# The full-width products of a transformer layer: 544 rows as 272 + 272 columns in place of 256 + 288

## The chip, the cores and the metric

The kernel runs on one core of a Trainium2 chip. The metric is the device time of one execution in microseconds (us); the time before is the median of three runs. Engines: TensorE (PE; its weight loads are shown apart as PEld), VectorE (DVE), ScalarE (ACT), GpSimd (POOL) and SyncE (SP), which issues most transfers.

## The reference

One layer of a model is computed for two inputs: a prompt of 512 rows and a sample of 8 sequences with 4 new rows each, 544 rows of 1024 features in all. Cut to what matters:

```python
def layer_forward(h, lp, conv_buf, ssm_h0, attn_fn, mem_k, mem_v):
    u = rmsnorm(h, lp['ffn1_pre_g'])
    h = h + 0.5 * rmsnorm(swiglu(u, lp['ffn1_wg'], lp['ffn1_wu'], lp['ffn1_wd']), lp['ffn1_post_g'])
    u = rmsnorm(h, lp['mix_pre_g'])
    z, xbc, dt_raw, q, k, v, qi, ki, wi, g_ssd, g_att = jnp.split(u @ lp['w_in'], IN_OFFSETS, axis=-1)
    y_ssd, new_conv, new_ssm = ssd_branch(z, xbc, dt_raw, ...)     # state-space branch
    y_att = attn_fn(q, k, v, qi, ki, wi)                           # sparse attention
    merged = (jax.nn.sigmoid(g_ssd) * (y_ssd @ lp['w_br_ssd'])
              + jax.nn.sigmoid(g_att) * (y_att @ lp['w_br_att']))
    h = h + rmsnorm(merged @ lp['w_out'], lp['mix_post_g'])
    u = rmsnorm(h, lp['mem_pre_g'])
    h = h + rmsnorm(mem_attend(u, lp['w_mq'], mem_k, mem_v) @ lp['w_mo'], lp['mem_post_g'])
    u = rmsnorm(h, lp['ffn2_pre_g'])
    h = h + 0.5 * rmsnorm(swiglu(u, lp['ffn2_wg'], lp['ffn2_wu'], lp['ffn2_wd']), lp['ffn2_post_g'])
    return h, (k, v, ki, new_ssm, new_conv)
```

All values are 32-bit floats. Nearly all arithmetic is in the products of `u` (or of the hidden layer, or of a branch) with a weight matrix.

## The kernel before

Activations lie feature-major: 128 features on the partitions, the T = 544 rows along the free axis (columns 0 to 511 the prompt, 512 to 543 the sample). A product with a weight matrix is made of tiles of 128 output features. For precision each operand is kept as two parts, high (`uh`, `wh`) and low (`ul`, `wl`), and a product is the sum of three: high by high, low by high, high by low.

`weights` (line 243) loads a part of a weight matrix through SyncE's queue into one of three raw buffers `wr`, ScalarE makes the high part `wh` (line 262) and VectorE or GpSimd the low part `wl` (line 263); there are two buffers of each. `mm` (line 275) makes one tile of a product: for each of its KT blocks of 128 input features, for each of the three pairs of parts, it issues one matmul per entry of `outs` (line 294). With `half=None` that is all 544 rows in two matmuls that go to a PSUM tile named `pg`; with `half` 0 or 1 it is rows 0 to 255 or 256 to 543 (`HALF`, line 21) in one matmul, into a tile named `pgh`. Every matmul has its own weight load in the instruction stream. `mm` is a generator: it yields an estimate of TensorE's time, 0.68 us per two blocks and entry of `outs`, by which `weave` (line 97) chooses whose instructions are emitted next; the emitted order is each engine's order.

Products by halves are used where a norm or a residual bounds two stages, so that one half can go on while the other is finished: the first six tiles of each feed-forward's up part, the last part of its down product, the first columns of `w_in`, and `w_out`, `w_mq`, `w_mo`. Full-width products are all the rest: most of the feed-forwards (lines 584, 585, 593), and of `w_in` (lines 727, 742, 993, 1115, 1140), `w_br_att` (line 1600) and `w_br_ssd` (line 1625). What reads a full-width result takes it whole: VectorE (`g`, lines 553 and 556; `y`, line 1601; `gt`, line 1626; `zt`, line 1118) or ScalarE (`y`, line 594; `th`, line 995; `CB`, line 1143 and others). The operands of full-width products are written in whole rows, or, at the head of a feed-forward and of the mixing stage, in the two halves of `HALF`, the second half by a generator that ends before the full-width products begin.

Of the kernel before, what the change touches and what calls it, by code (L numbers as in the profile page):

```python
# [14 lines left out]
PSUM = bass.MemoryType.PSUM  # L15
DRAM = bass.MemoryType.DRAM
P = 128
T = 544          # 512 prompt rows, then 32 of the sample
TP = 512
HA = 256         # the two halves of the rows: 0..255 and 256..543  # L20
HALF = ((0, 256), (256, 288))
D = 1024
# [7 lines left out]
def consts():  # L30
    """constants that depend on shapes alone"""
    a = np.arange
# [16 lines left out]
    # sample indexer; partitions (b, seg, t) with seg = pgh * 2 + c2  # L49
# [7 lines left out]
    # rows (c2, pgh, t, h); cols (pgh', c2', t')  # L57
# [3 lines left out]
    # rows (b4, t, h); cols (half, b', t')  # L61
# [35 lines left out]
def weave(*gens, extra=()):  # L97
    """emit streams side by side, the first the most urgent; each yields the tensor engine's time for what it has
    emitted, with the time until its next step can run where that is later, or WAIT for a flag; extra: streams
    that go on elsewhere when the others have ended"""  # L100
    now, idle = 0.0, 0
    live = [[g, 0.0] for g in (*gens, *extra)]
    while any(x[0] in gens for x in live):
        s = next((x for x in live if x[1] <= now), None)
        if s is None:
            s = min(live, key=lambda x: x[1])
            now = s[1]
        try:
            v = next(s[0])
        except StopIteration:  # L110
            live.remove(s)
            idle = 0
            continue
        if v is WAIT:
            idle += 1
            assert idle < 10000, "a wait that nothing ends"
            s[1] = now + 0.3
            continue
        idle = 0
        c, d = v if isinstance(v, tuple) else (v or 0.0, 0.0)  # L120
        now += c
        s[1] = now + d
# [38 lines left out]
class Net:  # L161
# [42 lines left out]
    def params(self):  # L204
        """gains and convolution parameters, feature on partitions"""
# [35 lines left out]
    WB = 2  # L241

    def weights(self, key, parts, KT, lo_eng=None):
        """parts: DRAM views [K, c]; -> hi, lo [P, KT, W] with hi + lo the weights"""
        nc, wp = self.nc, self.wp
        if key in self.wcache and self.wcount - self.wcache[key][0] < self.WB:
            return self.wcache[key][1]
        W = sum(p.shape[1] for p in parts)
        n = KT * W
        assert n <= 2048  # L250
        hi = wp.tile([P, 2048], F32R, tag="wh", name="wh", bufs=self.WB)
        lo = wp.tile([P, 2048], F32R, tag="wl", name="wl", bufs=self.WB)
        for k0, k1 in ((0, (KT + 1) // 2), ((KT + 1) // 2, KT)):
            raw = wp.tile([P, 1024], F32, tag="wr", name="wr", bufs=3)
            rv = raw[:, :(k1 - k0) * W].rearrange("p (k c) -> p k c", c=W)
            c = 0
            for p in parts:
                w = p.shape[1]
                nc.sync.dma_start(rv[:, :, c:c + w], p[k0 * P:k1 * P].rearrange("(k q) c -> q k c", q=P))
                c += w  # L260
            s, r = slice(k0 * W, k1 * W), raw[:, :(k1 - k0) * W]
            nc.scalar.copy(hi[:, s], r)  # L262
            (lo_eng or nc.vector).tensor_tensor(lo[:, s], r, hi[:, s].bitcast(F32), op=ALU.subtract)  # L263
        v = lambda t: t[:, :n].rearrange("p (k c) -> p k c", k=KT)
        self.wcache[key] = (self.wcount, (v(hi), v(lo)))
        self.wcount += 1
        return self.wcache[key][1]
# [7 lines left out]
    def mm(self, w, xs, c0, m=P, half=None):  # L275
        """one m-tile of weights.T @ x; half None: [m, T], else [m, rows of the half]"""
# [3 lines left out]
        if half is None:  # L280
            ps = self.pg.tile([P, 1024], F32, tag="pg", name="pg")
            outs = [(ps[:m, 256:512], 0, 256), (ps[:m, 512:800], 256, 288)]
            res = ps[:m, 256:800]
# [22 lines left out]
    def rsqrt(self, y, x, xh, t):  # L306
        """y = x ** -0.5 by Newton steps from a guess by the exponent"""
# [9 lines left out]
    def rms(self, sqs, inv_n, pool):  # L317
        """sqs: tiles [P, T] whose sum over tiles and partitions is the sum of squares
        -> rsqrt(mean + eps) on every partition, [P, rows of the prompt] and [P, rows of the sample] in PSUM"""
# [33 lines left out]
    def bound(self, half, sq, post_g, pre_g, rt=None):  # L353
        """hT += rms(y) * post_g, then u = rms(hT) * pre_g in two parts, on one half; sq: sum of squares of y;
        with rt, u goes without the rows' factor, which is left there for what is made of u"""
# [32 lines left out]
    def rms_h(self, acc, half):  # L388
        """as rms, for squares [P, rows of the half]"""
# [17 lines left out]
    def spread(self, y, half):  # L407
        """a factor by row, [P, blocks], on every partition, [P, rows of the half]"""
# [12 lines left out]
    def load_x(self, xp):  # L421
        """the rows, with the gains and the first weights of the feed-forward between the halves"""
# [16 lines left out]
    def load_T(self, half):  # L439
        """one half of x, feature-major; u without the rows' factor, and that"""  # L440
# [42 lines left out]
    def row_norm(self, x, scratch, pool):  # L483
        """rows of x [P, 2, D] over their root mean square"""
# [10 lines left out]
    def turn_rows(self, x, hi, lo, g):  # L495
        """[P, 2, D] times g, feature-major in two parts"""
# [10 lines left out]
    def memory_kv(self, mp):  # L507
        """-> the normed memory, then a piece for each of the weights' parts"""
# [28 lines left out]
    def ffn(self, nm, tail, lead, side=None, pieces=(), rt=None):  # L537
        """u -> y with hT += ... by tail(half, sq); lead: generator that completes u on half 1; side: a stream beside,
        pieces: streams that use the weights' buffers; rt: the factor of u's rows, if it is not in u"""
# [77 lines left out]
    def key_T(self):  # L617
# [4 lines left out]
        # pages of (b, pg16) in two halves  # L622
# [28 lines left out]
    def mix(self, lead):  # L651
# [28 lines left out]
        def outs(c):  # L680
            """weights and, per m-tile, (column, size, target)"""
# [88 lines left out]
    def out_rows(self, xT, n, out_p, out_s, pool, tag="orow"):  # L770
        """[n, T] feature-major -> rows of the outputs"""
# [14 lines left out]
    def dt_part(self, dw, ap):  # L786
        """step sizes, decays and their sums"""
# [28 lines left out]
        # softplus(x) = max(x, 0) + 2 atanh(e / (2 + e)), e = exp(-|x|)  # L816
# [16 lines left out]
        # prompt: sums within a chunk, [t, (c, h)]  # L833
# [21 lines left out]
        # sample; its rows three times over  # L855
# [32 lines left out]
        # d_skip by (h2, p)  # L888
# [14 lines left out]
    def sample_scores(self, qiT, kiT, dw):  # L903
# [8 lines left out]
        # indexer queries, block-diagonal over the two halves  # L912
# [9 lines left out]
        # head weights  # L922
# [15 lines left out]
        # new keys  # L938
# [87 lines left out]
    def prompt_att(self, kT, kx, V, qT, bias, g2, ready, wp):  # L1026
        """key groups 2 gp + g2"""
# [81 lines left out]
    def ssd_z(self, g):  # L1109
        """2 silu(z)"""  # L1110
# [11 lines left out]
    def ssd_x(self, g):  # L1122
        """x, B and C after the convolution"""
# [41 lines left out]
    def ssd_y(self, g, z):  # L1165
# [3 lines left out]
        # prompt  # L1169
# [37 lines left out]
        # sample; three copies of the rows for the products of the parts  # L1207
# [24 lines left out]
        # states of the prompt  # L1232
# [12 lines left out]
        # sample: states, feature-major, and their part of y; new states  # L1245
# [44 lines left out]
        # y  # L1290
# [41 lines left out]
    def conv_rows(self):  # L1332
        """last rows of the convolution's input"""
# [16 lines left out]
    def sample_select(self):  # L1350
# [17 lines left out]
        # threshold: the largest value that at least 256 of a query's candidates reach, two bits at a time in the  # L1368
        # floats' order; with the sign known a step turns the same bits of the float itself
# [32 lines left out]
        # rows in the pools  # L1402
# [16 lines left out]
        # new keys: row 65536 + j  # L1419
# [12 lines left out]
        # a query's list: its four lists end to end, each a run that starts so that its first entry falls in place  # L1432
# [29 lines left out]
    def sample_att(self):  # L1462
# [15 lines left out]
        def rows(st, v, q8):  # L1478
            """the keys or values of a query; the gathers run ahead"""
# [10 lines left out]
        for st in range(4):  # L1490
            # queries: [(g2, d), gp, (b, t), 2 x 16 heads], zero but for the heads of g;
            # tile kq holds heads 2 kq, 2 kq + 1 in its two halves; they read group kq // 2
# [79 lines left out]
    def att_in(self):  # L1572
        """y of the attention into the operands' place"""
# [15 lines left out]
    def att_out(self):  # L1589
        """B and its gate"""  # L1590
# [13 lines left out]
    def merge(self, h_d, rest):  # L1604
        """A with its gate and B, as the operands of w_out"""
# [27 lines left out]
    def project(self, name, post_g, pre_g, side=None, extra=()):  # L1633
        """u @ w, then its norm, residual and the next norm; half 1 of that is returned as a generator"""
# [18 lines left out]
    def mem(self):  # L1653
# [15 lines left out]
        def turn(out, mk):  # L1669
            """[256 m in 2 tiles, 1024] -> [P, 8, 256 m]"""  # L1670
# [8 lines left out]
        def soft(ps):  # L1679
            """softmax of ps / 16 over the free axis"""  # L1680
# [70 lines left out]
        def sample():  # L1751
            # rows (b, h, t)
            psS = self.pg.tile([P, 1024], F32, tag="pg", name="psS")[:, :256]
            # values: a part of y, buffers of the keys, and those of the prompt when it is done
# [107 lines left out]
def result(gen):  # L1862
    """run a generator to its end and return its value"""
# [12 lines left out]
# name, shape within the program, shape returned  # L1876
# [24 lines left out]
```

## Time and profile before

| | |
|---|---|
| median of 3 runs | 2350.27 us (2347.22 to 2356.14) |
| span of the profiled execution | 2361.3 us |
| instructions | 41404, of them 16615 matmuls with 16615 weight loads |
| busy: TensorE, its weight loads | 2254.3 us (95%), 2043.6 us (87%) |
| busy: VectorE, ScalarE, GpSimd | 1384.9 us (59%), 951.7 us (40%), 470.5 us (20%) |
| mean granted clock of TensorE | 0.973 of full speed |
| read from and written to memory | 270.84 MB, 37.48 MB |

The recorded duration of a matmul includes the time it takes to run through the array, so that successive ones overlap in the record. The distance from one start to the next is what one costs in a stream. The chain that ended last follows the work back from the last instruction, each step to what released it.

### The profile page before, as it was taken

Reading aid. Unit: us, or ns where it says so; the run is one execution under the profiler, and the core shown is the slowest. Engines: PE = TensorE matmul, PEld = TensorE weight load, DVE = VectorE, ACT = ScalarE, POOL = GpSimd, SP = SyncE. Lnnn points to the kernel's source line nnn. Section 1 sums busy time; section 2 is a strip of 40 time slices with the busy share of each in tenths; the row PEclk is TensorE's granted clock in tenths of the full one; section 3 lists DMA queues with packets and bytes.
Section 4 is the critical chain, followed back from the end, with each engine's and each line's share of the span. In section 5 each row is a group of like instructions: output and inputs, shape, how many; then the busy total and the mean of one; then the engine's idle time right before and its main releaser. Section 6 shows DMA issues by size and latency. Waiting matters only on the chain.

```text
span 2361.3 us, 41404 instructions
## 1 busy us (share of the span) xinstructions
PE 2254.3 (95%) x16615; PEld 2043.6 (87%) x16615; DVE 1384.9 (59%) x2996; ACT 951.7 (40%) x1725; POOL 470.5 (20%) x579
## 2 busy tenths in 40 slices
PE   7999999989999999989999999999999989999998
PEld 6999999978796678867777999999887688999997
DVE  6543334675798969856465777554763277423455
ACT  5333353445426563333433445232444244222232
POOL 0000010242132012266644111012420141000012
PEclk9999999989899999999999999999999999999998
DMA  6424564556422232454543444564452435233343
GB/s 188 150 82 147 156 214 145 151 162 193 149 86 71 64 103 63 135 153 143 154 142 101 138 126 146 156 199 152 152 170 97 154 85 156 84 97 90 94 122 106
DMA packets 326638, 311.56 MB, mean 132 GB/s; under 512 B 22505, under 2 KB 298089, under 8 KB 324373
## 3 DMA queue, kind: packets, MB, share of 16 engines
q1 hardware_dynamic: 316908, 282.28, 39.2%
q0 software_dynamic: 8576, 25.31, 3.5%
q8 instruction: 131, 2.15, 0.4%
q10 hardware_dynamic: 960, 1.31, 0.2%
q14 instruction: 63, 0.51, 0.1%
HBM read 270.84 MB, written 37.48 MB: 131 GB/s over the span
## 4 chain that ended last, share of the span: by engine, by line
PE 73%; DVE 14%; DMA 4%; ACT 3%; issue 3%; POOL 2%; SPq 0%; DVEq 0%; POOLq 0%; ACTq 0%
PE pg L294 38%; PE pgh L294 13%; PE pmo L528 2%; DVE wl L263 2%; PE psS L1514 2%; PE ppv L1064 1%; DMA wr<-in_ffn_wu 1%; ACT wh L262 1%; PE pys L1267 1%; PE psS L1772 1%; PE pO L1555 1%; PE poS L1800 1%; DVE acc L1020 1%; PE pqk L1041 1%; DVE IX L983 1%
## 5 line engine op out<-in xcount | busy, mean ns | idle before, releaser
L262 ACT CAST wh<-wr 128x1024 fp32r<-128x1024 f32 (+2 forms) x382 | 360.9, 960 | 542.1 <-PE pg L294 294.6
L263 DVE TENSOR_TENSOR wl<-wr,wh 128x1024 fp32r<-128x1024 f32 (+2 forms) x358 | 417.0, 1177 | 211.4 <-ACT wh L262 205.2
L294 PE MATMUL pg<-uh,wh 128*128 128x256 f32 (+1 forms) x2336 | 506.4, 296 | 1.6 <-DVE zt L1118 0.9
L294 PE MATMUL pg<-uh,wl 128*128 128x256 f32 (+1 forms) x2336 | 500.4, 294 | 0.0
L294 PE MATMUL pg<-ul,wh 128*128 128x256 f32 (+1 forms) x2336 | 498.6, 293 | 0.0
L294 PEld LDWEIGHTS pg<-uh,wh 128*128 128x128 f32 x2336 | 384.7, 192 | 20.6 <-issue 16.3
L294 PEld LDWEIGHTS pg<-uh,wl 128*128 128x128 f32 x2336 | 382.8, 191 | 8.7 <-issue 7.9
L294 PEld LDWEIGHTS pg<-ul,wh 128*128 128x128 f32 x2336 | 383.6, 192 | 6.2 <-issue 5.2
L294 PE MATMUL pgh<-uh,wl 128*128 128x256 f32 (+1 forms) x880 | 258.9, 297 | 14.4 <-DVE wl L263 14.1
L294 PE MATMUL pgh<-uh,wh 128*128 128x256 f32 (+2 forms) x880 | 260.6, 298 | 3.3 <-ACT uh L302 2.0
L294 PE MATMUL pgh<-ul,wh 128*128 128x256 f32 (+1 forms) x880 | 256.5, 293 | 1.0 <-DVE ul L303 0.6
L294 PEld LDWEIGHTS pgh<-uh,wl 128*128 128x128 f32 x880 | 168.5, 192 | 19.9 <-DVE wl L263 18.6
L351 POOL TENSOR_TENSOR sqf<-sqf,sqt 128x256 f32<-128x256 f32 (+1 forms) x56 | 62.0, 1108 | 617.1 <-ACT sqt L350 617.1
L294 PEld LDWEIGHTS pgh<-uh,wh 128*128 128x128 f32 (+1 forms) x880 | 169.7, 194 | 8.2 <-ACT uh L302 2.6
L294 PEld LDWEIGHTS pgh<-ul,wh 128*128 128x128 f32 x880 | 170.1, 194 | 2.5 <-DVE ul L303 1.3
L294 PE MATMUL pgh<-hh,wh 128*128 128x288 f32 (+1 forms) x352 | 101.8, 289 | 0.0
L294 PE MATMUL pgh<-hl,wh 128*128 128x288 f32 (+1 forms) x352 | 101.2, 287 | 0.0
L294 PE MATMUL pgh<-hh,wl 128*128 128x288 f32 (+1 forms) x352 | 101.0, 287 | 0.0
L1155 DVE SCALAR_TENSOR_TENSOR XO<-CB,convw,XO 128x600 f32<-128x600 f32 x96 | 83.5, 870 | 25.2 <-ACT XO L1153 24.8
L634 POOL DMA_INDIRECT G<-in_cache_kidx,ix x16 | 16.4, 1023 | 368.0 <-DVE ix L629 286.1
L263 POOL TENSOR_TENSOR wl<-wr,wh 128x1024 fp32r<-128x1024 f32 x24 | 57.6, 2410 | 138.1 <-ACT wh L262 85.2
L553 DVE TENSOR_TENSOR g<-pg,rt 128x544 f32<-128x544 f32 x32 | 23.2, 725 | 101.4 <-PE pg L294 101.4
(589 smaller groups left out, 4094.1 us busy)
## 6 DMA issues: line engine op xcount, KB each, us to landing
wr<-in_w_in SPq DMA_DIRECT2D x68, 512.0 KB
wr<-in_ffn_wg SPq DMA_DIRECT2D x52, 512.0 KB
wr<-in_ffn_wu SPq DMA_DIRECT2D x52, 512.0 KB
wr<-in_ffn_wd SPq DMA_DIRECT2D x46, 384.0 KB
wr<-in_ffn_wd SPq DMA_DIRECT2D x46, 320.0 KB
kt_d<-KT SPq DMA_DIRECT2D x8, 1024.0 KB
KT<-kt_d SPq DMA_DIRECT2D x8, 1024.0 KB
wr<-in_w_in SPq DMA_DIRECT2D x32, 256.0 KB
```

Of the source, the lines that this page charges most:

```text
L262: nc.scalar.copy(hi[:, s], r)
L263: (lo_eng or nc.vector).tensor_tensor(lo[:, s], r, hi[:, s].bitcast(F32), op=ALU.subtract)
L294: nc.tensor.matmul(o, a[:, k, c0:c0 + m], x[:, r0:r0 + n], start=(k == 0 and j == 0), stop=(k == KT - 1 and j == 2))
L351: nc.gpsimd.tensor_tensor(acc[:, :n], acc[:, :n], s[:, :n], op=ALU.add)
L528: nc.tensor.matmul(ps[:, :256], a[:, k, i * P:(i + 1) * P], b[:, k, :], start=(k == 0 and j == 0), stop=(k == 7 and j == 2))
L983: nc.vector.max_index(self.IX[:, r * 8:(r + 1) * 8], v, self.S)
L1020: nc.vector.match_replace(acc[:, :W], m8, acc[:, :W], IMM)
L1041: nc.tensor.matmul(ps[:, :W], qT[hb:hb + 64, h // 2, i * P:(i + 1) * P], ks[hb:hb + 64, gp, :W], start=True, stop=True)
L1064: nc.tensor.matmul(ps[g2 * 64:(g2 + 1) * 64, :], V[:, j, g * 64:(g + 1) * 64], PT[:, j, :], start=(j == 0), stop=(j == i))
L1155: nc.vector.scalar_tensor_tensor(xo, CB[:, j:j + 600], cw(j), xo, op0=ALU.mult, op1=ALU.add)
L1267: nc.tensor.matmul(ys[:, i * 64 + b * 4:i * 64 + b * 4 + 4], hTs[n][:, b4, :], XS[3][:, b * 4:b * 4 + 4], start=True, stop=True)
L1514: nc.tensor.matmul(psS[cg:cg + 32, :288], qz[:, gp, q8, :], KTs[q8 % 2][:, gp, :], start=False, stop=(q8 % 2 == 1 and gp == 1))
```

## The change

In `mm`, for `half=None`, the two matmuls of a step take columns 0 to 271 and 272 to 543 in place of 0 to 255 and 256 to 543. The result lies in columns 240 to 783 of the PSUM tile in place of 256 to 799; the two parts still meet at column 512. Comments are left out throughout, with line numbers kept; that is no change of the program.

```diff
         if half is None:
             ps = self.pg.tile([P, 1024], F32, tag="pg", name="pg")
-            outs = [(ps[:m, 256:512], 0, 256), (ps[:m, 512:800], 256, 288)]
-            res = ps[:m, 256:800]
+            outs = [(ps[:m, 240:512], 0, 272), (ps[:m, 512:784], 272, 272)]
+            res = ps[:m, 240:784]
         else:
```

`HALF` and with it the products by halves stay as they are.

## Rows read from the trace of the kernel before

**Rows 1.** The page's busy time by engine, and the granted clock of the core.
```profile
PE 2254.3 (95%) x16615; PEld 2043.6 (87%) x16615; DVE 1384.9 (59%) x2996; ACT 951.7 (40%) x1725; POOL 470.5 (20%) x579
core 0: 2361.3 us, clock 0.973
```

**Rows 2.** The page's chain that ended last, shares by engine and by line.
```profile
PE 73%; DVE 14%; DMA 4%; ACT 3%; issue 3%; POOL 2%; SPq 0%; DVEq 0%; POOLq 0%; ACTq 0%
PE pg L294 38%; PE pgh L294 13%; PE pmo L528 2%; DVE wl L263 2%; PE psS L1514 2%; PE ppv L1064 1%; DMA wr<-in_ffn_wu 1%; ACT wh L262 1%; PE pys L1267 1%; PE psS L1772 1%; PE pO L1555 1%; PE poS L1800 1%; DVE acc L1020 1%; PE pqk L1041 1%; DVE IX L983 1%
```

**Rows 3.** Instructions of tile pg (ns min/median/max); then two of the page's costliest groups.
```profile
L294 PE MATMUL pg<-uh,wh x2336: 276/293/610, 103.4 to 2272.0; 128*128 128x256 f32 x195
...
L294 PE MATMUL pg<-hh,wl x352: 274/288/378, 164.2 to 2139.9; 128*128 128x256 f32 x176
L294 PE MATMUL pg<-yh,wh x256: 279/293/442, 1536.1 to 1636.4; 128*128 128x256 f32 x126, 128*128 128x288 f32 x2
...
L294 PEld LDWEIGHTS pg<-uh,wl 128*128 128x128 f32 x2336 | 382.8, 191 | 8.7 <-issue 7.9
...
L553 DVE TENSOR_TENSOR g<-pg,rt 128x544 f32<-128x544 f32 x32 | 23.2, 725 | 101.4 <-PE pg L294 101.4
```

**Rows 4.** In order of time from 102.89 us: start us, us, engine, line, operation, operands.
```profile
102.89 0.19 PEld L294 LDWEIGHTS pgh<-uh,wh 128*128 128x128 f32 x1
...
103.02 0.19 PEld L294 LDWEIGHTS pgh<-ul,wh 128*128 128x128 f32 x1
103.16 0.29 PE L294 MATMUL pgh<-ul,wh 128*128 128x288 f32 x1
...
103.29 0.30 PE L294 MATMUL pgh<-uh,wl 128*128 128x288 f32 x1
...
103.42 0.42 PE L294 MATMUL pg<-uh,wh 128*128 128x256 f32 x2
...
103.67 0.41 PE L294 MATMUL pg<-ul,wh 128*128 128x256 f32 x2
```

**Rows 5.** The chain in order of time: start us, us, what, in how many instructions.
```profile
2014.25 258.57 PE pg L294 x2064
2272.82 34.80 PE pgh L294 x294
...
2314.11 14.68 PE pgh L294 x111
```

**Rows 6.** TensorE in order of time at half clock; last, windows with the granted clock.
```profile
946.40 0.66 PE L294 MATMUL pg<-uh,wl 128*128 128x256 f32 x2
946.85 0.66 PE L294 MATMUL pg<-uh,wh 128*128 128x256 f32 x2
...
1699.29 0.41 PE L294 MATMUL pgh<-ul,wh 128*128 128x256 f32 x1
1699.50 0.41 PE L294 MATMUL pgh<-uh,wl 128*128 128x256 f32 x1
...
1915.91 0.44 PE L294 MATMUL pgh<-ul,wh 128*128 128x288 f32 x1
1916.15 0.44 PE L294 MATMUL pgh<-uh,wl 128*128 128x288 f32 x1
...
942.50:949.20 6.70, 6.70 (x32) 0.50 0.54 146
```

**Rows 7.** Waits of TensorE: us in total, times, longest us.
```profile
PE pg L294 <- ACT yh L302: 3.2, 2, 2.6
...
PE pgh L294 <- ACT uh L302: 2.0, 2, 1.5
```

**Rows 8.** Window of the last feed-forward: us, busy PE, PEld, DVE, ACT, POOL; clock.
```profile
2014.30:2272.00 257.70, 257.70 (x2059) 257.70 (x2058) 96.04 (x117) 66.78 (x92) 0.00 (x0) 1.00 0.30 90
```

**Rows 9.** Weight loads in order of time in a stream of 256-column products.
```profile
2301.01 0.19 PEld L294 LDWEIGHTS pgh<-hl,wh 128*128 128x128 f32 x1
2301.13 0.19 PEld L294 LDWEIGHTS pgh<-hh,wl 128*128 128x128 f32 x1
```

## The prediction, on record before the run

> **What bounds the kernel now.** I read the page first. TensorE is busy for 95% of the span, VectorE for 59%, ScalarE for 40% [rows 1]: the reader is to see that only one engine is nearly full. A share of busy time can still be spent beside something slower, so next comes the chain that ended last: TensorE holds 73% of it, and the full-width products (tile `pg`, line 294) alone 38%, the products on one half of the rows (`pgh`, same line) another 13% [rows 2]. 38% of 2361.3 us is 897 us. The change touches `pg` alone.
>
> How many instructions is that? The groups of `pg` by operand count 2336, 352 and 256, each three times over (high by high, low by high, high by low) [rows 3]: 3 x 2944 = 8832 matmuls, half of them of 256 columns and half of 288, thus 4416 pairs. The duration in those rows (274 to 610 ns, median about 290) is no price: a matmul is pipelined, and the next one starts long before this one's recorded end. In order of time one sees it: a 288-column instruction starts every 0.13 us although each is drawn 0.29 us long, and a pair of `pg` starts every 0.25 us although it is drawn 0.41 us long [rows 4]. So the price of an instruction is the distance from start to start, and it is best read where the chain runs through hundreds of them in a row with nothing else between [rows 5]:
> - 256 and 288 in turn (`pg`): 258.57 us for 2064, 125.28 ns each, 250.6 ns a pair;
> - 256 alone (`pgh`, first half, last feed-forward): 34.80 us for 294, 118.4 ns each;
> - 288 alone (`pgh`, second half): 14.68 us for 111, 132.3 ns each.
>
> 8832 x 125.3 ns is 1107 us of TensorE; 897 us of it stands on the chain, or some 7160 instructions (897 / 0.1253). The other fifth lies beside other limits, where TensorE idles afterwards anyway. The lever is therefore plain: one nanosecond more or less on each full-width instruction moves the end by 7.2 us.
>
> **The change, part by part.** *The columns.* The number of matmuls, of weight loads, of columns and of products stays. Each pair of 256 + 288 becomes 272 + 272. If the price is a straight line in the number of columns, nothing happens, whatever its slope and its constant. Three lengths would be needed to see a bend, and the trace has only two for this kind of operand. What it does have is two tests. First, alone and in turn give the same: 118.4 + 132.3 = 250.7 ns against the measured 250.6 [rows 5]. So an instruction costs what its own length asks, and the unequal neighbours cost nothing extra that equal ones could save. Second, at half the clock (granted 0.50 in the window around the pair's rows, thus the 1.2 GHz level) a pair of `pg` starts every 0.45 us, 288 alone every 0.24 and 256 alone every 0.21 us [rows 6]; that is 0.24 and 0.213 us, 288 and 256 columns at 1.2 GHz, and again the pair is the sum. At this level the columns alone set the pace.
>
> At the full clock 256 columns at 2.4 GHz would be 106.7 ns and 288 would be 120.0, so 11.7 and 12.3 ns are added by something. Bounds for 272 follow from what that is. A constant on top of the columns: 118.4 + 6.7 = 125.1 ns from the short one, 132.3 - 6.7 = 125.6 from the long one. A factor on the columns: 118.4 x 272/256 = 125.8, 132.3 x 272/288 = 124.9. So 272 lies between 124.9 and 125.8 ns and I take the middle of the two lengths, 125.3, against 125.28 now: zero. The ends are worth -0.4 x 7160 = -2.9 us and +0.5 x 7160 = +3.6 us.
>
> *The first instruction's rows.* It reads rows 0 to 271, so it now needs the first 16 rows of the second half, which other instructions write. What would wait: TensorE is in order, so all that is behind it. But its partner, the next instruction, already needs rows 256 to 543, and the full-width products of the feed-forward begin 0.13 us after products of the second half, with the same operand [rows 4]; elsewhere the operands are written over all 544 rows at once. Zero; the cover is that order. Were the cover gone, the price is at the size of the waits of TensorE for operands in the table of waits: 2.0 us in two waits for `uh` and 3.2 us in two for `yh` [rows 7], the latter on full-width operands and so there already. The other way round, a writer of the first half that must wait for its readers waits for the first of a pair, which still ends before the second.
>
> *The end of a product.* The last instruction has 272 columns in place of 288. VectorE and ScalarE wait for the end of a product (`g` after `pg` 101.4 us, 32 instructions [rows 3]); that end comes 16 columns, 6.7 ns, nearer to the start of its last instruction, which itself starts 7 ns later. Zero. The consumers read as many elements, 544, from columns 240 to 783 of the tile in place of 256 to 799; the two parts still meet at column 512. I price that at zero: nobody on the chain waits long for them. If the reads became slower by a tenth, 0.07 us of the 0.725 us of `g` would lie beside two further products, and only the last product ahead of a stop would show it: under 2 us.
>
> *The order of work.* `mm` yields the same figure for its length, so `weave` emits the same order; no DMA, no queue and no weight buffer is moved. The loads ahead of a product, whose arrival does set the end in the halves of the feed-forward, start when a weight buffer comes free, that is when a product ends: unchanged to a few ns.
>
> *The clock.* The mean granted clock is 0.973 [rows 1]: 0.027 x 2361 = 64 us of full-clock time are lost in short stretches at half. These lie around stops that the change does not touch, but they move by themselves, and a tenth of them is 6 us. I count no trend and +-6 us for the range.
>
> **Sum:** 0 (bounds -3 and +4 from the columns, +2 from waits and reads, +-6 from the clock). The profiled execution spans 2361.3 us, 0.5% above the median of the runs, 2350.27; the sum is a difference, and zero of the one is zero of the other. Forecast 2350 us. The three runs lie between 2347.22 and 2356.14, so a change of 0.5% (12 us) is about what can be told from none; it would need 1.6 ns on every instruction.
>
> **The rivals.** *A. Weight loads hold the short instruction (faster).* Every matmul has a weight load of its own, and in the long full-width stretch the row of loads is busy for 257.70 of 257.70 us [rows 8]. Were 118 ns the time that a load needs, then 256 columns are below that floor, 272 would cost little more than 256, and 288 alone pays for its columns: up to 125.3 - 118.4 = 6.9 ns x 7160 = 49 us less, 2301 us. Against it: a load is drawn 191 ns long on average [rows 3], 190 ns beside either length [rows 4, 9], yet in the stream of 256 columns one starts every 0.12 us [rows 9] and in that of 288 every 0.13 us [rows 4], so it follows the columns; and the 288-column stream, which leaves a load 14 ns more, carries the same excess of 12 ns. Chance 0.05. The Trainium skill, Perfetto Trace Analysis, section Identifying the Most-Contended Engine, says to judge TensorE by the busy share of weight loads and not by matmul busy time. By that rule a row of loads at 100% would be the limit, and this rival would be the likeliest; the rows just named speak against taking it so here, since the loads stretch with the columns.
>
> *B. Starts and lengths inside a block of 32 columns cost the whole block (slower).* All moving operands on line 294 now start at column 0 or 256 and are 8 or 9 blocks of 32 columns long. 272 is 8.5 blocks, and the second instruction starts in the middle of one and touches half of it and 8 more. Nothing on the page has such a start, so nothing excludes it. If a touched block costs as much as a full one, both instructions cost 9 blocks, 132.3 ns: 7.0 x 7160 = +50 us, 2400 us. If only the odd start is charged, half of that: 2375 us. It decides at any charge above 1.6 ns an instruction. For it: the 12 ns that the columns don't explain at full clock, whose origin the trace doesn't show. Against: at half clock the columns explain all. Chance 0.09 in both sizes together.
>
> *C. It does not do what it says.* The products could have been limited elsewhere, so that even a bend in the price goes nowhere. With 38% of the chain in `pg` [rows 2] that would hold only for a bend of a nanosecond; it gives 2350 us as well, and I count it with the forecast.
>
> **How the numbers follow.** No change, by the straight line or by C: 0.84; A: 0.05, B: 0.09; some 0.02 for a shift of the clock's stretches by more than 12 us. The range takes the forecast's own bounds, -3 - 6 downward and +4 + 2 + 6 upward, and a small charge by B of half a nanosecond to a whole one: 2341 to 2364 us. Full A and B stay outside. Faster by over 0.5%: 0.06 (A and a little of the clock). Slower by over 0.5%: 0.11 (B and the waits). Within: 0.83.
>
> **What would show it.** In the trace after, `pg` has one form, 128x272, 8832 times; in the long full-width stretch of the last feed-forward 2064 instructions again take 258 to 259 us, start to start 125 ns and equal in a pair. Under 120 ns is A, with loads every 118 ns. 129 ns or more is B; if the two of a pair differ, the odd start is what costs. `pgh` must keep 118 and 132 ns, and the waits of TensorE their places. The forecast is wrong if the 2064 take 255 us or less, or 262 us or more, or if a wait for `uh` appears in front of the first instruction of full-width products.

## The result, and the profile after

The changed kernel takes 2364.36 us (median of 20 runs, 2352.96 to 2370.88), the kernel before 2351.53 us in the same company (20 runs, 2344.2 to 2358.77): ratio 1.0051, 95% interval 1.0036 to 1.0065. It is slower by half a percent, 12.8 us, where no change was forecast, and 0.4 us above the top of the range.

The page of after (busy us, share and instructions by engine; then the chain by line):

```profile
PE 2253.5 (95%) x16615; PEld 2042.3 (86%) x16615; DVE 1385.2 (59%) x2996; ACT 951.7 (40%) x1725; POOL 471.5 (20%) x579
PE pg L294 39%; PE pgh L294 14%; PE pmo L528 2%; DVE wl L263 1%; PE ppv L1064 1%; PE pys L1267 1%; PE psS L1514 1%; PE psS L1772 1%; PE pO L1555 1%; PE poS L1800 1%; DVE acc L1020 1%; ACT wh L262 1%; PE pqk L1041 1%; DVE V L982 1%; DVE IX L983 1%
```

The span and granted clock of the core in after:

```profile
core 0: 2363.8 us, clock 0.973
```

The instructions of tile `pg` in after (ns, min/median/max; where they begin and end, us):

```profile
L294 PE MATMUL pg<-uh,wh x2336: 282/287/596, 103.4 to 2274.4; 128*128 128x272 f32 x195
L294 PE MATMUL pg<-ul,wh x2336: 282/287/593, 103.7 to 2274.6; 128*128 128x272 f32 x195
```

Beside [rows 1 to 3] nothing stands out: the same number of instructions, busy times within 1.3 us, nearly the same chain. The one form of `pg` is there as forecast. The long stretches of the chain, start us, us, what, in how many instructions, answer [rows 5]:

```profile
2017.71 257.45 PE pg L294 x2064
2275.15 35.06 PE pgh L294 x294
...
2316.69 14.67 PE pgh L294 x111
```

257.45 us for 2064 full-width instructions are 124.73 ns each, against 125.28 before: 272 columns are not dearer than the mean of 256 and 288, they are 0.55 ns cheaper in this mean. As a mean, the straight line of the forecast holds. So the reader must ask where 12.8 us come from, if the thing that was changed became no slower. And there is a second oddity: the two profiled executions differ by 2.5 us alone (2361.3 and 2363.8), since that of before was slower than every one of the 20 timed runs of before. One trace of a program whose executions spread over 15 us is not the typical one; the experiments below run both kernels again.

What the two programs differ in beside the widths shows when their instructions are laid side by side, engine by engine, by name. `weave` emits them in the same order, as forecast. But the layer that turns the emitted instructions into the queues of the engines puts them in an order of its own, by its own estimates of how long each takes. In the program of before, 4918 of TensorE's 15316 instructions already stand at another place than the one at which they were emitted. (The page counts 16615 matmuls because some instructions are recorded as two.) The emitted order being the same, the two programs can differ only through the columns that this layer sees:

```
engine   instructions   at another place in the order of after
PE          15316         1171
DVE          2750          364
ACT          1646           93
SP            701           36
POOL          575           15
```

All of it lies between 290 and 1560 us, where several streams are woven together; the feed-forwards and everything from `w_out` on stand as before. So two theories: the widths (W), or the order (O).

### The profile page after: what moved, and what is told of

Read it like the earlier page. It is cut to its first block, busy times and chain, and to the rows that moved or that the text cites. A ratio compares the mean times of both kernels' runs of the same rounds, so it can differ in the third digit from the quotient of the medians.

```text
span 2363.8 us, 41404 instructions
## 1 busy us (share of the span) xinstructions
PE 2253.5 (95%) x16615; PEld 2042.3 (86%) x16615; DVE 1385.2 (59%) x2996; ACT 951.7 (40%) x1725; POOL 471.5 (20%) x579
## 4 chain that ended last, share of the span: by engine, by line
PE 75%; DVE 14%; issue 3%; ACT 3%; DMA 3%; POOL 2%; SPq 0%; DVEq 0%; POOLq 0%; ACTq 0%
PE pg L294 39%; PE pgh L294 14%; PE pmo L528 2%; DVE wl L263 1%; PE ppv L1064 1%; PE pys L1267 1%; PE psS L1514 1%; PE psS L1772 1%; PE pO L1555 1%; PE poS L1800 1%; DVE acc L1020 1%; ACT wh L262 1%; PE pqk L1041 1%; DVE V L982 1%; DVE IX L983 1%
## 5 line engine op out<-in xcount | busy, mean ns | idle before, releaser
L294 PE MATMUL pg<-uh,wh 128*128 128x272 f32 x2336 | 504.4, 295 | 1.7 <-DVE zt L1118 1.0
L294 PE MATMUL pg<-ul,wh 128*128 128x272 f32 x2336 | 498.9, 293 | 0.0
L294 PE MATMUL pg<-uh,wl 128*128 128x272 f32 x2336 | 497.1, 294 | 0.0
L294 PEld LDWEIGHTS pg<-uh,wh 128*128 128x128 f32 x2336 | 373.1, 191 | 18.8 <-issue 14.7
L294 PEld LDWEIGHTS pg<-ul,wh 128*128 128x128 f32 x2336 | 373.6, 191 | 10.1 <-issue 8.9
L294 PEld LDWEIGHTS pg<-uh,wl 128*128 128x128 f32 x2336 | 372.4, 192 | 7.8 <-issue 7.3
```

Source lines behind the costliest of these rows:

```text
L294: nc.tensor.matmul(o, a[:, k, c0:c0 + m], x[:, r0:r0 + n], start=(k == 0 and j == 0), stop=(k == KT - 1 and j == 2))
```

## Experiments: the width or the order

Both can be had apart. The program is built once with one width, the order of each engine's instructions is read off, and it is built again with the other width and with that order kept by edges between neighbours on each engine (issue order alone, no waits):

```diff
+    nc, arrays, traced = build(inputs, ORDER)                       # width whose order is wanted
+    nc, arrays, _ = build(inputs, WIDTH, order_of(nc, traced))      # width that runs
...
+            for names in order.values():
...
+                for a, b in zip(names, names[1:]):
+                    tc.add_manual_dep(traced[b], a, how, reason="order")
```

The kernel before once more:

> The kernel before once more, for its own spread and its granted clock. The profiled execution of before spanned 2361.3 us, above all of its 20 timed executions (2344 to 2359), so its trace may not be a typical one. Theory O (the order of instructions): a typical execution shows about 2351 us and fewer half-clock stretches between 900 and 1330 us than the trace of after has there (48 us). Theory W (the width): no prediction of its own, 2351 us.

272 + 272 in the order of before (`WIDTH, ORDER = 272, 256`):

> 272 + 272 columns, but every engine's instructions kept in the order of the kernel before. Theory W (a 272-column instruction costs more, in the array or through the clock): as slow as after, ratio 1.005, about 2364 us. Theory O (the widths are worth -0.7 ns an instruction on most full-width products and +2 ns on those of w_br_ssd, about -4 us in all, and the loss is in the changed order): ratio 0.998, about 2347 us.

256 + 288 in the order of after (`WIDTH, ORDER = 256, 272`):

> 256 + 288 columns, but every engine's instructions in the order that after has. Theory W: ratio 1.000, about 2351 us. Theory O: the whole loss and the few us that the width gives back, ratio 1.006 to 1.008, 2365 to 2370 us.

The changed kernel once more:

> The changed kernel once more, in the same company as the three others. Both theories: ratio 1.005, 2364 us. Theory O: by executions, the time goes with the granted clock (0.977 at 2353 us, 0.970 at 2369 us were seen).

Measured on one chip, which is a little slower than the first (before: 2361.11 us, 23 runs):

| width | order of before | order of after |
|---|---|---|
| 256 + 288 | 2365.15 us, 1.0014 (0.9998 to 1.0030) | 2377.85 us, 1.0070 (1.0051 to 1.0089) |
| 272 + 272 | 2366.72 us, 1.0017 (1.0004 to 1.0030) | 2377.30 us, 1.0067 (1.0048 to 1.0086) |

Down a column the width changes, along a row the order. The width is worth 1.6 us in one order and -0.6 us in the other, less than the 4 us by which one and the same program differs from itself here (2361.11 and 2365.15). The order is worth 12.7 us with the old width and 10.6 us with the new. Theory W falls as the cause of the 12.8 us; O stands. The small gain of the widths that O had added (-4 us, ratio 0.998) did not come: e2 is at 1.0017. The granted clocks of the executions say where it went. An execution's time multiplied by its granted clock is an estimate of its time at full clock. By the means of 12 executions each, it is 3.5 us less in e2 than in e1, and the slower clock (0.9734 against 0.9754) takes 4.8 us back. The latter is only about twice its standard error, so whether the width itself lowers the clock stays open.

The chains show how exactly the price of the widths repeats in the long stretch, and that it is not one price everywhere. That of e1, the kernel before:

```profile
2013.84 258.57 PE pg L294 x2064
2272.41 34.80 PE pgh L294 x294
```

That of e2, the new width in the old order:

```profile
1557.67 81.45 PE pg L294 x641
...
2013.84 257.45 PE pg L294 x2064
```

That of e4, the changed kernel again:

```profile
1573.73 82.85 PE pg L294 x652
...
2031.22 257.45 PE pg L294 x2064
```

258.57 with the old width in both executions, 257.45 with the new in three. The products with `w_br_ssd` (at 1557 us in e2, 1573 us in e4, operands `yh` and `yl`) go the other way: 81.45 / 641 = 127.1 ns with 272 columns, where the chain of the first profile of before has 80.10 us for as many, 125.0 ns:

```profile
1556.89 80.10 PE pg L294 x641
```

The long stretch hides two prices of its own. It is 480 products with `uh` and `ul`, 528 with `hh` and `hl`, and again 1056 with `uh` and `ul`. Of the 528, the groups that start first and last, before and then after:

```profile
L294 PE MATMUL pg<-hh,wh x176: 278/286/298, 2074.4 to 2139.4; 128*128 128x256 f32 x88, 128*128 128x288 f32 x88
L294 PE MATMUL pg<-hh,wl x176: 277/288/297, 2074.9 to 2139.9; 128*128 128x256 f32 x88, 128*128 128x288 f32 x88
...
L294 PE MATMUL pg<-hh,wh x176: 285/288/288, 2077.3 to 2142.9; 128*128 128x272 f32 x176
L294 PE MATMUL pg<-hh,wl x176: 289/290/290, 2077.8 to 2143.4; 128*128 128x272 f32 x176
```

From the first start to the last that is 65.5 us before and 66.1 us after. In the traces, start to start, these products went from 124.4 to 125.6 ns and those with `uh` and `ul` around them from 125.6 to 124.5 ns. The 0.55 ns are the mean of a gain of 1.1 ns on three quarters of the products and a loss of 1.1 ns on the rest.

## Experiments: where in the order

The changed order was then put in by thirds, with the old width: each engine's list is taken from the order of after in one part and from that of before in the rest, cut where both have put the same instructions behind them.

```diff
+CUTS = [{"PE": 5870, "DVE": 903, ...},          # at about 875 us
+        {"PE": 7313, "DVE": 1451, ...}]         # at about 1150 us
...
+    FROM = (272, 256, 256)                      # e5; e6: (256, 272, 256); e7: (256, 256, 272)
```

> 256 + 288 columns; the order of after up to about 875 us (projections, prompt attention and gates), the order of before from there on. If the loss were made wherever the order changed, a third of it would be here: ratio 1.003. From the traces of the two orders, which lose nothing against each other up to 890 us (the order of after is even some 7 us ahead there, by fewer half-clock stretches near 500 and 640 us, which may be chance): ratio 1.000, 2359 to 2366 us.

> 256 + 288 columns; the order of after from about 875 to 1150 us alone (selection and attention of the sample beside the first groups of the state-space branch). In the traces the order of after loses 12.8 us between 890 and 1100 us, with 48 us at half clock in place of 24. Theory S2 (the loss is made here): ratio 1.004 to 1.006. Theory S3 (it is made later): 1.000. If the trace shows the extra half-clock time but no extra waits, the clock carries it.

> 256 + 288 columns; the order of after from about 1150 us on alone (rest of the state-space branch, products of w_br_att and w_br_ssd). In the traces the order of after loses 5.2 us between 1430 and 1485 us, with 13.7 us at half clock in place of 3.4; but the first trace of before shows that half-clock stretch too, so it may come and go. Theory S3: ratio 1.002 to 1.004. Theory S2: 1.000.

Against 2348.34 us of before (29 runs): the first third 2348.65 us, 0.9996 (0.9980 to 1.0013); the middle 2357.90 us, 1.0035 (1.0020 to 1.0051); the last 2354.88 us, 1.0024 (1.0005 to 1.0043). 0.9996 x 1.0035 x 1.0024 is 1.0055, between the two measurements of the whole (1.0051, 1.0067). The first third has a quarter of the changed places and costs nothing; the middle costs 8 us and the last some 6 us.

What does the middle third cost, waits or clock? The same 1202 matmuls (the first and the last of them are the same instructions in both) take in e5, with the order of before there (the window, its us, busy TensorE with the count of its instructions, granted clock, share of the DMA engines, GB/s):

```profile
894.80:1082.00 187.20, 169.86 (x1201) 0.97 0.42 122
```

and in e6, with the order of after there:

```profile
894.10:1093.10 199.00, 178.41 (x1202) 0.92 0.39 116
```

11.8 us longer in these two executions. TensorE is idle for 17.3 us in the one and for 20.6 us in the other, 3.3 us more; the other 8.5 us are the same work done in more time, at a granted clock of 0.92 in place of 0.97. The two orders of the first set of runs say the same; e1, the kernel before:

```profile
897.90:1093.00 195.10, 175.41 (x1202) 0.94 0.40 118
```

and e3, the old width in the order of after:

```profile
890.60:1098.50 207.90, 185.54 (x1202) 0.89 0.37 111
```

10.1 us more of busy time and 2.7 us more idle. So in these executions about a quarter of the loss is waiting and three quarters are the slower clock that goes with it. All executions together say much the same: the mean granted clock is 0.9762 in e6 and 0.9788 in before, and 0.0026 of 2350 us is 6 us of a mean loss of 7.9 us. Which of the instructions moved in this third do it was not tried. TensorE's clock is granted at 0.89 to 0.97 in these windows, with 17 to 22 us of stops in each, and at 1.00 throughout the long stretch without a stop [rows 8]. The Trainium skill, TensorE: Matmul & The Clock Gate, section The HAM clock gate, says that activity of TensorE releases a throttle which is there by default; the rows just named agree in kind.

## Experiments: one place

In the last third, the trace of e7 has a half-clock stretch of 10 us at one place. TensorE in order of time, in brackets how long it was idle and for whom:

```profile
1457.46 0.52 PE L294 MATMUL pg<-ul,wh 128*128 128x256 f32 x2
...
1458.82 0.52 PE L294 MATMUL pg<-uh,wh 128*128 128x256 f32 x2
1459.25 1.53 PE L1236 MATMUL pst<-xe,Bt 128*128 128x256 f32 x6
1461.25 0.70 PE L1236 MATMUL pst<-xe,Bt 128*128 128x256 f32 x2 [0.47 <-ACT H L1239]
1462.47 0.66 PE L1253 MATMUL ph<-ident,h 128*128 128x128 f32 x4 [0.52 <-DVE Bs L1227]
1464.13 0.52 PE L294 MATMUL pg<-uh,wh 128*128 128x256 f32 x2 [1.00 <-DVE zt L1118]
1464.48 0.95 PE L1253 MATMUL ph<-ident,h 128*128 128x128 f32 x4
1465.09 0.82 PE L294 MATMUL pg<-ul,wh 128*128 128x256 f32 x2
1465.71 0.66 PE L294 MATMUL pg<-uh,wl 128*128 128x256 f32 x2
```

Three stops, 2.0 us together, and behind them a pair of `pg` starts after 0.62 us, where 0.25 us is its pace. The windows before and in the slow stretch of e7 (columns as above):

```profile
1455.00:1464.60 9.60, 7.61 (x51) 1.00 0.71 230
1464.60:1474.80 10.20, 10.20 (x49) 0.50 0.00 0
```

10.2 us at the 1.2 GHz level, so some 5 us lost for 2 us of stops. In the order of before more full-width matmuls stand between the transposes of a group (lines 1178 to 1211) and the state products (line 1236): 16 in place of 12; six of them were moved from behind the transposes to ahead of them. This one place was tried alone:

```diff
+    BASE, OTHER, A, B = (256, 272, 9231, 9336)      # e8: order of before, the place as in after
+    BASE, OTHER, A, B = (272, 256, 9231, 9336)      # e9: order of after from 1150 us on, the place as in before
...
+            mixed[e][A:B] = orders[OTHER][e][A:B]   # for TensorE
```

> 256 + 288 columns, the order of before everywhere but for one place on TensorE: 105 instructions of one group of the state-space branch (lines 1178 to 1275) stand as after has them, so that six full-width products come ahead of the group's transposes in place of behind them, where they lie beside TensorE's waits. Theory place (these six decide whether TensorE's clock falls for some 10 us at about 1465 us): ratio 1.002 to 1.0025, the half-clock stretch at 1465 us in the trace. Theory whole (the stretch is lost by the many small shifts together, or by VectorE's and the queues' order): 1.000, no such stretch.

> 256 + 288 columns, the order of after from about 1150 us on, but at that one place TensorE's order of before. Theory place: ratio 1.000, no half-clock stretch at 1465 us. Theory whole: 1.002, with the stretch.

> 256 + 288 columns, the order of after from about 1150 us on, as measured once at 1.0024 (1.0005 to 1.0043), here beside the two others. Both theories: 1.002, with a half-clock stretch of about 10 us at 1465 us.

Against 2352.76 us of before (29 runs): e8 2358.11 us, 1.0027 (1.0014 to 1.0041); e9 2350.80 us, 1.0001 (0.9981 to 1.0022); e10 2358.17 us, 1.0028 (1.0012 to 1.0044). So 105 of TensorE's 15316 instructions, 61 of them at another place, carry what the last third costs: put in alone they cost all of it, and without them the rest of that third costs nothing that can be measured. Theory place holds in the times. In the traces it does not: those of e8 and e10 show no half-clock stretch there, though theory place expected one in both. The profiled execution of e8 was its fastest (2348.23 us, where its 11 others took 2354 us or more); that of e10 was an ordinary one (2357.64 us, the median is 2358.17):

```profile
1448.00:1458.00 10.00, 7.97 (x52) 1.00 0.48 159
1458.00:1468.00 10.00, 10.00 (x85) 1.00 0.01 2
```

This is e8, the same stops just before (2.0 us idle of 10) and the full clock behind them. And e10:

```profile
1460.00:1470.00 10.00, 8.02 (x53) 1.00 0.48 163
1470.00:1480.00 10.00, 10.00 (x85) 1.00 0.09 26
```

In the six traces with the order of after at this place the 10 us at half clock are there four times; in the six with that of before once, in the trace on which the prediction was made. Six and six are too few to show that the place changes how often the clock falls there. The stops themselves differ little: over these 105 instructions TensorE idles for 2.0 to 2.2 us in the order of after and for 1.5 to 1.8 us in that of before. Without a half-clock stretch they take 19.7 us in the one and 18.8 to 19.3 us in the other, so the place costs less than 1 us directly.

The rest is clock, by the mean granted clock of all executions: 0.9761 in e8 and 0.9758 in e10, but 0.9782 in before and 0.9784 in e9. 0.0021 and 0.0024 of 2353 us are 5 and 6 us (standard error about 2 us), the whole of the mean loss of 5.5 us in either. So it is shown that these 105 places cost 5 to 6 us and that the granted clock goes with it. That the clock is lost in just this stretch is not shown; in the ordinary execution of e10 it was not.

## Why the prediction was wrong

*Columns:* right in the sum, too narrow in the bounds. The term was 0, between -2.9 and +3.6 us. The long stretch gives -0.55 ns an instruction, 7160 x 0.55 = 3.9 us less by the prediction's own multiplication; the products with `w_br_ssd`, 768 of the 8832, give 2.1 ns more, 1.6 us. Both lie outside the ends that were put (124.9 and 125.8 ns; measured 124.7 and 127.1), since the price goes with the operands, which the forecast priced as one. That the term still comes out near its lower end, because losses take back a part of the gains, is luck. In the times, order held fixed, the width is worth nothing that can be told from the noise (1.6 us, -0.6 us). None of the signs by which the forecast was to be known as wrong appeared (257.45 us lies between its 255 and 262): they test the width, and the order of work had no sign.

*The first instruction's rows, the end of a product:* right; no new wait in front of full-width products, and [rows 7] keep their places in the order of before.

*The order of work:* this step failed. It argued that `mm` yields the same figure and `weave` therefore emits the same order. That is so, and it is not the last word on the order: a scheduling layer stands behind it, whose estimates see the columns of each instruction. The text on the kernel before makes the same mistake where it calls the emitted order each engine's order. The edit of two lines moved 1171 of TensorE's instructions, and the changed order costs 12.7 and 10.6 us where the forecast put nothing. Nothing in the profile of before told of that, but the building of the program would have, and a sentence on this layer, with a price, belonged among the rivals.

*The clock:* this step failed with it. It said that the half-clock stretches lie around stops that the change does not touch, with no trend and +-6 us. But the order that the change moves decides what stands around these stops: 8.5 of the 11.8 us of the middle third are clock, and e3 against e1, by their mean granted clocks (0.9713 and 0.9754), loses 10 of 12.6 us through it, all one way. By executions, 0.977 goes with 2353 us and 0.969 with 2369 us in the 20 runs of after.

*The base:* the working was done on a trace of before that held the half-clock stretch at 1465 us, which the five other traces with that order lack. For a sum of zero that did not matter; for judging the clock it did.

*The range:* its upper end does not follow from its own terms. +4 + 2 + 6 us and half a nanosecond on 7160 instructions (3.6 us) give 2366 us and not 2364. That would have taken in the measured time, but by luck: the order of work is in none of these terms.

*Rivals:* A (the floor of weight loads, -49 us) and B (blocks of 32 columns, +50 us) did not come. B's charge of 7 ns is not in the rows, though its direction is in those with `yh` and `hh` (+2.1 and +1.1 ns). C, "it does not do what it says", was meant as a limit elsewhere; what came was that it does more than it says.

## What to carry to other kernels

Where a layer reorders instructions by estimated durations, an edit of one instruction's size is an edit of the order of everything woven beside it: lay the two programs' orders side by side before the columns are priced. To tell size from order, keep one and change the other; it takes four runs and leaves little to argue. Where TensorE's clock can fall, the price of a changed order is not only its waits: here the waits were about a quarter of it in the middle third and less at the one place. And a single trace does not show where the clock is lost on the average; the granted clock of every execution shows how much.

## What the runs showed of the hardware

A matmul of 272 columns has no single price in a stream. With `uh` it takes 124.5 ns and with `hh` 125.6 ns in the last feed-forward, with the operands of `w_br_ssd` 127.1 ns (e2 and e4), while 256 and 288 in turn cost 125.6, 124.4 and 125.0 ns in the mean at these places. The stretch of 2064 took the same 257.45 us in all three traces with 272 columns that are shown here. The runs don't show what makes the difference. And 2 us of stops were followed by 10.2 us at the 1.2 GHz level in e7 and by none in e8 and e10. Executions of one program on one chip spread over 12 to 21 us, the slower ones as a rule at the lower granted clock. What decides it from one execution to the next stayed open.
